# Moving the large SBUF buffers by 160 bytes, and the feed-forward's small pool behind its others, in a one-core streaming-encoder block

## The chip, the cores and the metric

The kernel runs on one core of one Trainium2 chip. The metric is the device time of one execution in microseconds (us). Before the change it is 2313.43 us, the median of three runs (2312.34 to 2315.29).

## The reference

One layer of an encoder trunk on a sequence of 1024 tokens of width 1024, all in fp32. A combined projection feeds two recurrent branches (RWKV-7 and HGRN2), whose gated sum is projected and added to the tokens; then come cross-attention to 256 memory tokens, a SwiGLU feed-forward with 2816 hidden columns, and a last norm. Cut to what the change touches:

```python
    h = h + (gate_a * y_a + gate_b * y_b) @ w_out[l]
    ...
    o = jnp.einsum('bhqm,bmhd->bqhd', p, v).reshape(B, S, D_MODEL)
    h = h + o @ xa_wo[l]

    u = rmsnorm(h, norm_ffn_g[l])
    h = h + (jax.nn.silu(u @ ffn_w1[l]) * (u @ ffn_w3[l])) @ ffn_w2[l]
return rmsnorm(h, norm_final_g)
```

## The kernel before, in words

**Products.** Each large product is taken with operands split into a high and a low part of type fp32r: `split` (L282 writes the high part on ScalarE, L286 the low part on GpSimd or VectorE). `mm3` (L299 to L302) issues three matmuls for each pair of blocks: high by high, low by high, high by low. In the profile an operation `P<-ah,whT` of L300 has the result P, the moving operand ah (512 columns of 4 bytes, so 2048 bytes of each partition) and the stationary operand whT (128 columns, 512 bytes). The mixing part's instructions are recorded through one helper, so they all stand at L103.

**Stages.** The mixing part (projections pproj, the two recurrences) takes the first 1300 us or so. Then come keys and values of the memory (pk, pvv), the output projection and cross-attention (pq, psc, po, pw) up to 1663 us, and from there the feed-forward with the final norm.

**End of attention.** `add_project` multiplies by `xa_wo`, adds the result to the tokens tok (VectorE, L1796), squares them for the next norm (ScalarE, L1799) and stores each of the last four token tiles to the scratch tensor h_d (L1801, a DMA that SyncE, SP, issues). These four tiles lie in 4096-byte buffers of attention's ring hp; the last buffer of that ring spans bytes 174,240 to 178,336 of each partition.

**Feed-forward.** The first layer's 2 x 2 block product is done with seven products instead of eight (P1 to P7) for each of 11 blocks f and the two matrices w1 and w3; one product is 12 matmuls (`product`). P5 and P4 of f = 0, 1 and 2 use only the first half of the tokens, which is normalized already, so they come right behind attention's last projection (`early_products`): 12 products, read as `P<-ah,whT`, `P<-al,whT` and `P<-ah,wlT`. Their weights come in 256-KB loads (`raw`, L1969, on SP's DMA queue) into the tile wraw, 10 buffers: 8 loads for each f, in the order A0[0], A1[0], A0[2], A1[2], ... (`weights(f, True)`). `behind` lets the scheduler set the loads of f = 0 no earlier than the eighth-last load of `xa_wo`, and those of f = 1 no earlier than the last. `early_operands` takes differences of them on VectorE (L2080, L2083, L2084) and splits each into whT (ScalarE, L282) and wlT (GpSimd, L286). The operand of the first product, T1[0], needs the loads 1 and 3. `late_blocks` loads the other half of the tokens back from h_d into hn (L1998), takes its norm (ssn: L1999 and `rstd`, L276 and L277; hn: L2003), and loads the sums s and b (L2005, L2006), before it transposes. The second layer (acc<-wh,th and the like) follows from the scratch tensors.

**Order.** The tile framework schedules the instructions of every engine by priorities and by its own estimate of when operands and buffers are free; each engine, and the SP queue, then works strictly in that order. A tile of a new pool that lies over a tile of a pool that was closed has to wait until that old tile's last use (the pools of `tpool` with `reuse_waits="tile"`).

**Addresses.** A pool gets its bytes when it is opened, behind the pools that are open. The moving operands of 2048 bytes start at these remainders of a division by 2048: uh, ah, whi and those of the same pools at 1888, the feed-forward's tl, th, wh and wl at 224. The stationary rows of 512 bytes start at 352 (the first group) and at 224 (the second) beyond a multiple of 512. The feed-forward's pools are opened in the order f_s (2432 bytes: ssn, ssf, junkf), f_t (tl, th), f_f (u2, u3, c, kept), f_w (wraw, wh, wl). Its first wraw buffer starts at byte 178,400, just behind the last buffer of attention's ring hp.

Of the kernel before, what the change touches and what calls it, by code (L numbers as in the profile page):

```python
# [10 lines left out]
F32 = mybir.dt.float32  # L11
# [7 lines left out]
P = 128  # L19
# [165 lines left out]
def tile_trunk(ctx, tc, x, mem, norm_mix_g, w_in, rw_mu, rw_w0, rw_w2, rw_a0, rw_a2, rw_g2,  # L185
# [5 lines left out]
    def tpool(**kw):  # L191

        return tc.tile_pool(reuse_waits="tile", **kw)

    const = ctx.enter_context(tc.tile_pool(name="const", bufs=1))
    dram = ctx.enter_context(tc.tile_pool(name="dram", bufs=1, space=DRAM))

    def behind(ins, name):

        tc.add_manual_dep(ins, name, mybir.DependencyInfo(mybir.DependencyClass.NoSync, mybir.DependencyReason.DATA),  # L200
                          reason="order")
# [137 lines left out]
    def scratch(name, shape):  # L339
        return dram.tile(shape, F32, name=name)  # L340
# [1615 lines left out]

    sp = ctx.enter_context(tpool(name="f_s", bufs=2))
    ring = ctx.enter_context(tpool(name="f_t", bufs=20))  # L1960
    fp = ctx.enter_context(tpool(name="f_f", bufs=2))
    wp = ctx.enter_context(tpool(name="f_w", bufs=1))
    pp = ctx.enter_context(tpool(name="f_p", bufs=8, space=PSUM))
    hd = scratch("hid_d", [FT, NHALF, P, HALF])
    hsd = scratch("hsum_d", [4, HF, P, HALF])
# [363 lines left out]
```

## Time and profile before

| what | value |
|---|---|
| median of three runs | 2313.43 us (2312.34 to 2315.29) |
| the profiled execution, first to last instruction (span) | 2308.0 us, 5.4 us below the median |
| TensorE (PE) busy | 2270.0 us, 98% of the span, 18,262 matmuls |
| VectorE, ScalarE, GpSimd busy | 68%, 49%, 45% |
| mean granted TensorE clock | 0.998 |
| PE in the 48 us up to 1665 us | 48.00 us busy |
| DMA share in the same 48 us | 0.98 of the 16 engines, 287 GB/s |
| loads of feed-forward weights (L1969) | 145, 256 KB each |

The time beside the span is read as a constant: what lies around the first and the last instruction. In a window's row stand the busy time of PE, PE's weight loads, VectorE, ScalarE and GpSimd with their instructions, then the granted TensorE clock, the share of time in which the 16 DMA engines moved data, and GB/s. In a row of the timeline stand the start, the duration, the engine, the line, the operation, the tiles and, in brackets, the idle time just before it and what ended it; for SP the duration is the time to issue the transfers. Matmuls are pipelined: each shows some 390 ns, but the next one starts some 230 ns later.

### The profile page before, as it was taken

Reading aid. Unit: us, or ns where it says so; the run is one execution under the profiler, and the core shown is the slowest. Engines: PE = TensorE matmul, PEld = TensorE weight load, DVE = VectorE, ACT = ScalarE, POOL = GpSimd, SP = SyncE. Lnnn points to the kernel's source line nnn. Section 1 sums busy time; section 2 is a strip of 40 time slices with the busy share of each in tenths; the row PEclk is TensorE's granted clock in tenths of the full one; section 3 lists DMA queues with packets and bytes.
Section 4 is the critical chain, followed back from the end, with each engine's and each line's share of the span. In section 5 each row is a group of like instructions: output and inputs, shape, how many; then the busy total and the mean of one; then the engine's idle time right before and its main releaser. Section 6 shows DMA issues by size and latency. Waiting matters only on the chain.

```text
span 2308.0 us, 47067 instructions
## 1 busy us (share of the span) xinstructions
PE 2270.0 (98%) x18262; PEld 1860.1 (81%) x18262; DVE 1558.0 (68%) x2513; ACT 1134.2 (49%) x2259; POOL 1037.3 (45%) x1129
## 2 busy tenths in 40 slices
PE   7999999999999999999999999999999999999998
PEld 5788887787888887888788888888888888888887
DVE  5788874666777757776766566555778665566655
ACT  6545454545565656564566424443453333334533
POOL 3555555555565655575566100000266655551212
PEclk9999999999999999999999999999999999999999
DMA  5444445233334244434334897117933433348653
GB/s 174 119 134 123 131 122 171 69 102 85 88 103 122 75 120 112 134 82 116 92 90 123 286 348 264 55 56 261 290 121 117 132 96 110 96 158 305 207 172 120
DMA packets 393691, 327.94 MB, mean 142 GB/s; under 512 B 107595, under 2 KB 318653, under 8 KB 392061
## 3 DMA queue, kind: packets, MB, share of 16 engines
q1 hardware_dynamic: 391549, 319.17, 45.4%
q0 software_dynamic: 1344, 4.72, 0.5%
q8 instruction: 144, 2.36, 0.4%
q10 hardware_dynamic: 576, 1.05, 0.1%
q14 instruction: 78, 0.64, 0.1%
HBM read 228.12 MB, written 96.21 MB: 141 GB/s over the span
## 4 chain that ended last, share of the span: by engine, by line
PE 73%; DVE 4%; DMA 3%; POOL 2%; issue 1%; ACT 1%; SPq 0%; POOLq 0%; ACTq 0%; DVEq 0%
PE pproj L103 21%; PE P L301 6%; PE P L302 6%; PE P L300 6%; PE acc L301 3%; PE acc L302 3%; PE acc L300 3%; PE pw L302 3%; PE pw L301 2%; PE pw L300 2%; PE cm L103 2%; PE psA L103 2%; PE psc L103 1%; PE po L103 1%; PE pq L301 1%
## 5 line engine op out<-in xcount | busy, mean ns | idle before, releaser
L103 PE MATMUL pproj<-uh,whi 128*128 128x512 f32 x768 | 320.0, 417 | 0.7 <-DVE q L103 0.7
L103 PE MATMUL pproj<-uh,wlo 128*128 128x512 f32 x768 | 300.9, 392 | 2.7 <-POOL wlo L103 2.3
L103 PE MATMUL pproj<-ul,whi 128*128 128x512 f32 x768 | 301.5, 393 | 0.0
L286 POOL TENSOR_TENSOR wl<-wraw,wh 128x512 fp32r<-128x512 f32 x87 | 121.4, 1402 | 199.8 <-ACT wh L282 171.7
L103 POOL TENSOR_TENSOR wlo<-wraw,whi 128x512 fp32r<-128x512 f32 x96 | 128.4, 1348 | 118.4 <-ACT whi L103 111.2
L300 PE MATMUL pproj<-uh,whi 128*128 128x512 f32 (+1 forms) x432 | 177.4, 411 | 1.1 <-ACT uh L328 0.7
L282 ACT ACTIVATE whi<-wraw 128x512 fp32r<-128x512 f32 (+1 forms) x166 | 100.9, 617 | 156.3 <-PE pw L302 73.6
L103 PEld LDWEIGHTS pproj<-uh,whi 128*128 128x128 f32 x768 | 144.5, 188 | 34.0 <-DVE q L103 2.0
L302 PE MATMUL pproj<-uh,wlo 128*128 128x512 f32 (+1 forms) x432 | 170.0, 394 | 1.8 <-POOL wlo L286 1.8
L103 PEld LDWEIGHTS pproj<-ul,whi 128*128 128x128 f32 x768 | 144.4, 188 | 32.3
L301 PE MATMUL pproj<-ul,whi 128*128 128x512 f32 (+1 forms) x432 | 169.6, 393 | 0.0
L103 PEld LDWEIGHTS pproj<-uh,wlo 128*128 128x128 f32 x768 | 145.0, 189 | 28.1 <-POOL wlo L103 2.8
L277 POOL TENSOR_TENSOR ss<-ss,nhalf 128x4 f32<-128x4 f32 (+1 forms) x7 | 6.2, 881 | 323.1 <-DMA wraw<-in_xa_wo_dram 186.6
L286 POOL TENSOR_TENSOR wlT<-wraw,whT 128x512 fp32r<-128x512 f32 x72 | 102.0, 1424 | 85.1 <-ACT whT L282 73.7
L282 ACT ACTIVATE wh<-wraw 128x512 fp32r<-128x512 f32 x143 | 87.0, 623 | 92.3 <-PE P L301 69.1
L286 DVE TENSOR_TENSOR wlo<-wraw,whi 128x512 fp32r<-128x512 f32 x134 | 93.1, 701 | 55.3 <-ACT whi L282 53.4
L103 ACT ACT_TABLE_LOAD x90 | 115.5, 1283 | 14.3 <-DVE m L103 7.2
L301 PE MATMUL acc<-wl,th 128*128 128x512 f32 x308 | 119.9, 389 | 0.0
L302 PE MATMUL acc<-wh,tl 128*128 128x512 f32 x308 | 119.8, 389 | 0.0
L300 PE MATMUL acc<-wh,th 128*128 128x512 f32 x308 | 119.8, 389 | 0.0
L2273 DVE TENSOR_TENSOR tl<-tl,th 128x512 fp32r<-128x512 f32 x77 | 60.1, 792 | 63.6 <-ACT th L2272 63.2
L300 PE MATMUL pw<-whi,ah 128*128 128x512 f32 x256 | 100.6, 393 | 1.2 <-ACT whi L282 0.7
(457 smaller groups left out, 6383.0 us busy)
## 6 DMA issues: line engine op xcount, KB each, us to landing
wraw<-in_w_in_dram SPq DMA_DIRECT2D x148, 256.0 KB
wraw<-in_ffn_w_dram SPq DMA_DIRECT2D x145, 256.0 KB
y<-in_ffn_w_dram SPq DMA_DIRECT2D x22, 512.0 KB
wsum_d<-y SPq DMA_DIRECT2D x11, 1024.0 KB
hsum_d<-s SPq DMA_DIRECT2D x44, 256.0 KB
tl<-hsum_d SPq DMA_DIRECT2D x44, 256.0 KB
wraw<-wsum_d SPq DMA_DIRECT2D x44, 256.0 KB
hid_d<-s SPq DMA_DIRECT2D x33, 256.0 KB
```

The costliest lines, as they stand in the source:

```text
L103: r = getattr(self.engine, op)(*a, **kw)
L277: nc.gpsimd.tensor_tensor(dst, tmp, nhalf[:, 0:n], op=ALU.pow)
L282: nc.scalar.activation(hi, src, AF.Copy)
L286: e.tensor_tensor(lo, src, hi.bitcast(F32), op=ALU.subtract)
L300: nc.tensor.matmul(ps, ah, bh, start=first, stop=False)
L301: nc.tensor.matmul(ps, ah, bl, start=False, stop=False)
L302: nc.tensor.matmul(ps, al, bh, start=False, stop=last)
L2273: tt(hl, hl.bitcast(F32), hh.bitcast(F32), op=ALU.subtract)
```

## The change

Two edits. A tile of 160 bytes named align, which nothing reads, is the first of the const pool, so that everything behind it moves up by 160 bytes: uh from byte 20,320 to 20,480, which is 10 times 2048. And the pool f_s is opened as the last of the feed-forward's four SBUF pools instead of the first, so that the three others begin 2432 bytes lower; with the 160 bytes that makes 2272 bytes: tl from 55,520 to 53,248, the first wraw buffer from 178,400 to 176,128, wh from 198,880 to 196,608. After it, of the 512-column moving operands those at 1888 and 224 lie at 0 beyond a multiple of 2048 (7620 matmuls of the program), and the stationary rows belonging to them at 0 beyond a multiple of 512. The last buffer of attention's ring hp now spans 174,400 to 178,496, and the first two wraw buffers (176,128 to 180,224) lie partly over it.

```diff
+    const.tile([P, 40], F32, name="align")
...
-    sp = ctx.enter_context(tpool(name="f_s", bufs=2))
     ring = ctx.enter_context(tpool(name="f_t", bufs=20))
     fp = ctx.enter_context(tpool(name="f_f", bufs=2))
     wp = ctx.enter_context(tpool(name="f_w", bufs=1))
+    sp = ctx.enter_context(tpool(name="f_s", bufs=2))
```

No instruction is added or removed, but the scheduler's order differs from about 1617 us on, and nowhere earlier. All lines behind L196 count two more after the change (L1969 becomes L1971).

The queue of SP at the end of attention's last projection, before the change: L1770 loads `xa_wo`, L1969 loads feed-forward weights, L1801 stores the tokens, L1998 loads them back.

```order
L1770 DMA wraw<-in_xa_wo_dram 128x512
L1969 DMA wraw<-in_ffn_w_dram 128x4x128 x8
L1770 DMA wraw<-in_xa_wo_dram 128x512 x6
L1823 DMA early_d<-sums 128x512
L1770 DMA wraw<-in_xa_wo_dram 128x512
L1969 DMA wraw<-in_ffn_w_dram 128x4x128 x8
...
L1969 DMA wraw<-in_ffn_w_dram 128x4x128 x6
L1801 DMA h_d<-tok 128x1024 x3
L1998 DMA hn<-h_d 128x512
L1801 DMA h_d<-tok 128x1024
L1998 DMA hn<-h_d 128x512 x7
```

Left out between the two pieces are the rest of 29 such weight loads (8, 8, 3, 2, 1, 1 and 6) and stores to early_d; all 29 stand ahead of the stores of the tokens.

The same place of the same queue after the change (L1772, L1971, L1803 and L2000 are those lines).

```order
L1772 DMA wraw<-in_xa_wo_dram 128x512 x8
L1825 DMA early_d<-sums 128x512
...
L1803 DMA h_d<-tok 128x1024 x3
L2000 DMA hn<-h_d 128x512
L1803 DMA h_d<-tok 128x1024
L2000 DMA hn<-h_d 128x512 x3
L1971 DMA wraw<-in_ffn_w_dram 128x4x128 x16
L2000 DMA hn<-h_d 128x512 x4
```

The first weight load of the feed-forward now stands behind all four stores of the tokens and behind four of the eight loads hn; its wait is for the third of those stores to have landed and for ScalarE's squares (L1799) of the last tiles.

VectorE at the same place before the change: L286 makes the last low parts of attention, L2080, L2083 and L2084 take the differences of weights (here those of f = 1; those of f = 0 stand further up), L1796 adds the projection to the tokens.

```order
L286 TENSOR_TENSOR al<-sums,ah 128x512
L2080 TENSOR_TENSOR wraw<-wraw 128x512 x2
L2083 TENSOR_TENSOR wraw<-wraw 128x512 x2
L2084 TENSOR_TENSOR wraw<-wraw 128x512 x2
L1796 TENSOR_TENSOR tok<-pw,tok 128x512 x4
L1999 TENSOR_REDUCE ssn<-ssq 128x4
L276 TENSOR_SCALAR ssn<-ssn 128x4
L2003 TENSOR_SCALAR hn<-hn,ssn 128x512 x8
```

And VectorE after the change.

```order
L288 TENSOR_TENSOR al<-sums,ah 128x512
L1798 TENSOR_TENSOR tok<-pw,tok 128x512 x4
L2001 TENSOR_REDUCE ssn<-ssq 128x4
L278 TENSOR_SCALAR ssn<-ssn 128x4
L2005 TENSOR_SCALAR hn<-hn,ssn 128x512 x4
L2082 TENSOR_TENSOR wraw<-wraw 128x512 x2
L2085 TENSOR_TENSOR wraw<-wraw 128x512 x2
L2086 TENSOR_TENSOR wraw<-wraw 128x512 x2
```

The differences of f = 0 and of f = 1 now stand behind the last additions to the tokens and behind four scalings of hn; ScalarE's splits into whT and GpSimd's into wlT have moved with them. PE's order is the same as before: the last matmul of pw, then the early products P.

## The prediction

> **What bounds the kernel now.** I read the page first: its busy times and the shares of the chain that ended last.
>
> ```profile
> span 2308.0 us, 47067 instructions
> PE 2270.0 (98%) x18262; PEld 1860.1 (81%) x18262; DVE 1558.0 (68%) x2513; ACT 1134.2 (49%) x2259; POOL 1037.3 (45%) x1129
> PE 73%; DVE 4%; DMA 3%; POOL 2%; issue 1%; ACT 1%; SPq 0%; POOLq 0%; ACTq 0%; DVEq 0%
> ```
>
> TensorE is busy for 98% of the span and carries 73% of the chain. So two things can move the time: how fast matmuls follow one another, and whether PE is left without operands. Next the busy times by stage: the end of attention, the hand-over to the feed-forward, and stretches of the feed-forward.
>
> ```profile
> 1617.00:1665.00 48.00, 48.00 (x228) 39.86 (x227) 38.61 (x56) 23.91 (x48) 12.02 (x8) 1.00 0.98 287
> 1665.00:1677.00 12.00, 12.00 (x53) 9.74 (x52) 5.49 (x11) 4.48 (x8) 6.18 (x5) 1.00 0.94 330
> 1677.00:1700.00 23.00, 23.00 (x117) 19.08 (x116) 16.34 (x24) 14.98 (x27) 15.49 (x11) 1.00 0.43 131
> 1700.00:1900.00 200.00, 199.08 (x874) 163.55 (x873) 146.96 (x170) 68.70 (x119) 124.73 (x88) 1.00 0.35 109
> 1900.00:2100.00 200.00, 200.00 (x877) 164.25 (x875) 116.24 (x149) 68.47 (x113) 101.26 (x77) 1.00 0.42 137
> ```
>
> PE has no gap across the hand-over (48.00 of 48, 12.00 of 12, 23.00 of 23), at full clock, while the DMA engines move 287 to 330 GB/s. From 1700 us on it is idle for 0.92 us in 400. So whatever PE loses at the hand-over is not caught up behind it: there is no later wait that would shrink.
>
> How the gap is avoided stands in the timelines: first SP's queue, then three rows of VectorE, then PE, ScalarE and GpSimd.
>
> ```profile
> 1617.57 7.03 SPq L1969 DMA_DIRECT2D wraw<-in_ffn_w_dram  x8
> 1634.65 5.79 SPq L1969 DMA_DIRECT2D wraw<-in_ffn_w_dram  x8
> 1653.94 6.02 SPq L1969 DMA_DIRECT2D wraw<-in_ffn_w_dram  x6
> 1660.19 2.15 SPq L1801 DMA_DIRECT2D h_d<-tok  x3
> 1665.09 0.32 SPq L1998 DMA_DIRECT2D hn<-h_d  x1
> 1665.50 0.38 SPq L1801 DMA_DIRECT2D h_d<-tok  x1
> 1665.94 4.37 SPq L1998 DMA_DIRECT2D hn<-h_d  x7
> ```
>
> ```profile
> 1640.56 0.69 DVE L2080 TENSOR_TENSOR wraw<-wraw 128x512 f32<-128x512 f32 x1 [2.27 <-DMA wraw<-in_ffn_w_dram]
> 1663.35 0.69 DVE L1796 TENSOR_TENSOR tok<-pw,tok 128x512 f32<-128x512 f32 x1 [1.35 <-PE pw L302]
> 1668.28 0.49 DVE L2003 TENSOR_SCALAR hn<-hn,ssn 128x512 f32<-128x512 f32 x1 [3.02 <-DMA hn<-h_d]
> ```
>
> ```profile
> 1662.91 0.40 PE L302 MATMUL pw<-whi,al 128*128 128x512 f32 x1
> 1663.15 0.40 PE L300 MATMUL P<-ah,whT 128*128 128x512 f32 x1
> 1665.94 0.39 PE L300 MATMUL P<-ah,whT 128*128 128x512 f32 x1
> ```
>
> ```profile
> 1665.97 0.63 ACT L282 ACTIVATE whT<-wraw 128x512 fp32r<-128x512 f32 x1 [1.11 <-PE P L301]
> 1666.68 1.29 POOL L286 TENSOR_TENSOR wlT<-wraw,whT 128x512 fp32r<-128x512 f32 x1 [0.27 <-ACT whT L282]
> ```
>
> Feed-forward weights are loaded 46 us ahead of use, beside attention's last projection, and the first early product starts at 1663.15, 0.24 us after the last pw. These early products were put there to fill the time in which h_d is stored, loaded back and normalized (1660.19 to past 1668.28).
>
> **The change part by part: the hand-over.** After the change all feed-forward weight loads stand on SP behind the four stores h_d and the first four loads hn, and VectorE, ScalarE and GpSimd have moved with them. PE's order is unchanged, so PE stands at the first P until the weights for it are loaded, subtracted and split. Queued behind the waiting SP instruction are 16 weight loads, four hn, then s and b; behind the waiting matmul is all of the feed-forward. Step by step:
>
> 1. The last add to the tokens ends at 1663.35 + 0.69 = 1664.04; it can't be earlier, as pw runs as before. The first hn waits for the first store to land. Before, that took 1665.09 − 1660.19 = 4.9 us, behind six weight loads issued up to 1659.96; an hn load itself takes 1668.28 − 1665.09 = 3.2 us from issue to use. So the first hn goes out at 1663.4 to 1665.1 and the fourth store at 1664.04 to 1665.5.
> 2. Behind it three hn (4.37 / 7 = 0.62 us each, 0.44 for the store): first weight load at 1666.3 to 1667.8. The first product needs loads 1 and 3, and a load takes 5.79 / 8 = 0.72 us to issue: load 3 at 1667.8 to 1669.2.
> 3. From issue to use: at least the 3.2 us of hn; at most what the third load of the batch at 1634.65 took to the subtraction at 1640.56, 4.5 us. That gives 1671.0 to 1673.7.
> 4. Subtraction 0.69 and split 0.63: PE starts at 1672.3 to 1675.0 instead of 1663.15, so it stands for 9.2 to 11.9 us.
> 5. The third matmul needs wlT, 1.29 us behind whT, of which two matmuls at half clock cover some 0.85; with the hand-over between engines 0.4 to 0.8 us.
>
> Standing has a price of its own, the clock. The one wait of PE over 2 us in the mixing part and the windows around it:
>
> ```profile
> 406.00 0.39 PE L103 MATMUL pproj<-uh,whi 128*128 128x512 f32 x1
> 408.04 0.39 PE L103 MATMUL pproj<-uh,whi 128*128 128x512 f32 x1
> 410.77 0.79 PE L103 MATMUL pproj<-uh,wlo 128*128 128x512 f32 x1 [2.34 <-POOL wlo L103]
> 411.00:415.00 4.00, 4.00 (x14) 3.25 (x15) 0.09 (x1) 1.34 (x3) 1.63 (x2) 0.60 0.72 150
> 415.00:425.00 10.00, 10.00 (x48) 8.28 (x47) 8.10 (x13) 9.52 (x16) 8.64 (x13) 1.00 0.53 130
> ```
>
> After 2.34 us of idling the clock is 0.60 over the next 4 us and 1.00 after them: 4 × 0.40 = 1.6 us lost. Here PE idles four times as long; I take 1.6 as the low end and twice that and a little, 3.4, as the high one, 2.0 as the value. The Trainium skill ("TensorE: Matmul & The Clock Gate", "What's actually happening") has the clock halved after an idle window of about 3.4 us and restored after as long a busy one; by that rule a window at half clock costs, as an estimate, 1.7 us, and the trace agrees in size, though here 2.34 us of idling sufficed.
>
> 6. The weights of f = 2 come later as well: 16 weight loads, 8 hn, and s and b are 32 transfers of 256 KB or 8.4 MB, 25 us at 330 GB/s, beside the 8 products of 12 × 232.5 ns that f = 0 and 1 give to cover it, 22 us. I take 0 to 4 us, 1.5 as the value, since before, the DMA engines were already at 0.94 in this stretch.
>
> Sum of what is added: low 9.2 + 0.4 + 1.6 + 0 = 11.2 us, high 11.9 + 0.8 + 3.4 + 4 = 20.1, and with the middle values 10.6 + 0.6 + 2.0 + 1.5 = 14.7.
>
> **The change part by part: the addresses.** What alignment does to a matmul must come from rows with operands that lie differently today.
>
> ```profile
> L300 PE MATMUL P<-ah,whT x176: 390/393/477, 1663.1 to 2084.3; 128*128 128x512 f32 x176
> L300 PE MATMUL P<-hB,wh x176: 389/389/495, 1700.0 to 2062.3; 128*128 128x512 f32 x176
> L698 PE MATMUL pg<-sgh,g2s x16: 391/394/497, 379.9 to 397.2; 96*128 96x512 f32 x16
> L300 PE MATMUL pk<-mT,whi x48: 277/283/283, 1305.6 to 1333.5; 128*128 128x256 f32 x48
> L103 PE MATMUL pproj<-uh,whi 128*128 128x512 f32 x768 | 320.0, 417 | 0.7 <-DVE q L103 0.7
> L300 PE MATMUL pproj<-uh,whi 128*128 128x512 f32 (+1 forms) x432 | 177.4, 411 | 1.1 <-ACT uh L328 0.7
> L300 PE MATMUL acc<-wh,th 128*128 128x512 f32 x308 | 119.8, 389 | 0.0
> L300 PE MATMUL pw<-whi,ah 128*128 128x512 f32 x256 | 100.6, 393 | 1.2 <-ACT whi L282 0.7
> ```
>
> And two matmuls of 256 columns, pk, with 24 more between them:
>
> ```profile
> 1330.21 0.28 PE L300 MATMUL pk<-mT,whi 128*128 128x256 f32 x1
> 1333.21 0.28 PE L301 MATMUL pk<-mT,whi 128*128 128x256 f32 x1
> ```
>
> The pace is the distance of starts: (408.04 − 406.00) / 9 = 226.7 ns for pproj, whose moving operand is at 1888 of 2048, and (1665.94 − 1663.15) / 12 = 232.5 ns for the early products. The one thing that sets the latter apart is that ah (1888) and whT (224) differ by more than a multiple of 256; hB and wh, both at 224, show a shorter duration, 389 instead of 393. So what these rows reward is that moving and stationary rows lie alike, which 224 with 224 and 1888 with 352 (both 96 beyond a multiple of 256) do already. After the change ah and whT are alike too: 528 matmuls (3 × 176) × 5.8 ns = 3.1 us gained. The bounds: 0 if it isn't the address, and 3.1 if it is; I take 3.1, since the two paces and the durations of these products fit it. For the others I take 0: they change from alike to alike.
>
> **Sum.** 14.7 − 3.1 = 11.6 us more; the bounds are 11.2 − 3.1 = 8.1 and 20.1. The profiled execution has a span of 2308.0, 5.4 us below the median of 2313.4 of the runs; the same 5.4 is put on the span after: 2308.0 + 11.6 + 5.4 = 2325.0 us, its own range 2319 to 2334 (the bounds of the sum, 2321.5 to 2333.5, and 2 us below).
>
> **The rivals.**
>
> *Aligned rows stream faster.* A moving row on a multiple of 2048 could be worth something in itself; this ends on the other side. pk starts every (1333.21 − 1330.21) / 25 = 120 ns; by the slope between 256 and 512 columns, 512 columns take (226.7 − 120) × 2 = 213.4 ns, so 13.3 ns of each matmul isn't columns. If that were rows crossing a boundary of 2048 bytes, it would be won back in the 3 × (768 + 432 + 308 + 256) + 1848 = 7140 matmuls (1848 for the first layer of the feed-forward: 11 × 7 × 2 products of 12): 95 us, for 2313.4 + 14.7 − 95 = 2233 us (the 3.1 are part of it). It overtakes the hand-over from 11.6 / 7140 = 1.6 ns a matmul on.
>
> Against it: a row of 256 columns, which crosses such a boundary half as often at most, keeps the same 13.3; offsets 224 and 1888 cross it at opposite ends of a row and run alike; and g2s, whose moving rows lie on multiples of 128, is no shorter (394). For it: no moving row of 512 columns lies on a multiple of 2048 today, so nothing shows the case itself. The Trainium skill ("TensorE: Matmul & The Clock Gate", "Back-to-back issue gap") gives N / 2.4 + 2.5 ns for matmuls alone, an estimate of 215.8 ns here; if alignment were what this kernel lacks to it, 10.9 × 7140 = 78 us would go and the time would be 2250; no run here shows a pace below 226.7, and the trace's weight load before each matmul is the simpler reason. Chance 0.16.
>
> *Aligned rows collide.* Moving and stationary rows that start at the same remainder of 2048, and those of the other engines too, might meet in the memory. Before, the spread from best to worst alike-ness was 5.8 ns; at 1 to 6 ns on 7140 matmuls that is 7 to 43 us, on top of the hand-over 2332 to 2368. For it only that addresses do matter (393 against 389); against it that pairs alike in the low 8 bits are the fast ones. Chance 0.07.
>
> *The hand-over is hidden after all, or the change does nothing.* If stores land at once and the weights arrive while the h_d work still runs, PE would stand for 3 us or less, with 3.1 gained from ah: 2311 to 2317. Against it is the order, which puts the weights behind the last add. Chance 0.05.
>
> **Chances.** The hand-over as worked out has 0.72: 2325.0. A difference of 0.2%, 4.6 us, is about what a measurement of this kernel can tell from none. Faster by more: the first rival and a trifle, 0.17. Within: the third rival and the low tail of the forecast, 0.08. Slower: 0.75. The range leaves out the first rival (0.16) and the far end of the second: 2311 (the third rival's low end) to 2348, which takes in a collision of up to 3 ns.
>
> **What would show it.** In the changed profile's timeline SP issues wraw<-in_ffn_w_dram only after 1664 us; PE's first `P<-ah,whT` carries an idle time of 9 to 12 us ended by ACT whT; the clock of the next 4 us is near 0.6; no other stage of PE idles more than before; early products show 389 instead of 393; and the ends of the mixing part and of attention keep their times. If pproj's starts are closer than 226.7 ns, or the feed-forward ends earlier though the idle time is there, the first rival holds and the forecast is wrong; if they are farther apart, the second.

## The result, and the profile after

The changed kernel takes 2329.4 us (median of five runs, 2328.04 to 2332.14) against 2312.34 for the kernel before (five runs); the ratio is 1.0078, with a 95% interval of 1.0067 to 1.0089, so some 18 us slower. The profiled execution has a span of 2327.3 us, 19.3 more than before. In the experiments below one of the eleven executions with 128 bytes alone took 7837.34 us; that kernel's ratio leaves it out.

The busy times by stage, in the windows that were shown of before (busy time of PE, weight loads, VectorE, ScalarE and GpSimd, then clock, DMA share and GB/s):

```profile
1617.00:1665.00 48.00, 46.22 (x220) 38.24 (x219) 24.33 (x39) 20.27 (x41) 1.01 (x1) 1.00 0.39 141
1665.00:1677.00 12.00, 1.91 (x4) 1.10 (x5) 5.39 (x9) 1.26 (x2) 3.03 (x3) 0.62 1.03 315
1677.00:1700.00 23.00, 23.00 (x98) 18.91 (x97) 18.15 (x20) 10.01 (x18) 10.57 (x8) 0.90 1.02 330
1700.00:1900.00 200.00, 194.39 (x855) 160.12 (x854) 150.88 (x169) 74.18 (x130) 133.43 (x91) 0.97 0.36 113
1900.00:2100.00 200.00, 200.00 (x884) 165.58 (x884) 126.41 (x155) 67.62 (x113) 111.12 (x84) 1.00 0.37 119
```

PE's 12 us from 1665 on, full before, hold 1.91 us of work at a clock of 0.62. The DMA engines are at 0.39 up to 1665 us, where they were at 0.98, and saturated behind it: the weights that came early now come late. The fourth row shows more: 194.39 busy instead of 199.08, at 0.97. There is a second wait behind 1700 us.

SP's queue (start, time to issue), and the first use of the weights on VectorE and on ScalarE:

```profile
1657.85 4.40 SPq L1803 DMA_DIRECT2D h_d<-tok  x3
1662.36 0.37 SPq L2000 DMA_DIRECT2D hn<-h_d  x1
1663.97 0.32 SPq L1803 DMA_DIRECT2D h_d<-tok  x1
1664.34 1.77 SPq L2000 DMA_DIRECT2D hn<-h_d  x3
1666.20 13.89 SPq L1971 DMA_DIRECT2D wraw<-in_ffn_w_dram  x16
```

```profile
1673.54 1.50 DVE L2082 TENSOR_TENSOR wraw<-wraw 128x512 f32<-128x512 f32 x2 [1.81 <-DMA wraw<-in_ffn_w_dram]
```

```profile
1674.27 0.63 ACT L284 ACTIVATE whT<-wraw 128x512 fp32r<-128x512 f32 x1 [9.51 <-DVE wraw L2082]
```

And PE: the first early product, its slow followers, nine matmuls at the new pace, the second wait, and a product well behind both.

```profile
1674.95 0.79 PE L302 MATMUL P<-ah,whT 128*128 128x512 f32 x1 [11.74 <-ACT whT L284]
...
1677.33 0.63 PE L303 MATMUL P<-al,whT 128*128 128x512 f32 x1
...
1680.74 0.63 PE L302 MATMUL P<-ah,whT 128*128 128x512 f32 x1
...
1681.55 0.39 PE L304 MATMUL P<-ah,wlT 128*128 128x512 f32 x1
1681.78 0.39 PE L302 MATMUL P<-ah,whT 128*128 128x512 f32 x1
...
1683.82 0.39 PE L302 MATMUL P<-ah,whT 128*128 128x512 f32 x1
...
1716.45 0.39 PE L304 MATMUL P<-hB,wl 128*128 128x512 f32 x1
1721.14 1.22 PE L302 MATMUL P<-hB,wh 128*128 128x512 f32 x2 [4.31 <-ACT hB L2023]
...
1724.94 0.79 PE L303 MATMUL P<-lB,wh 128*128 128x512 f32 x1 [1.30 <-DVE lB L2024]
...
1806.89 0.39 PE L302 MATMUL P<-hB,wh 128*128 128x512 f32 x1
```

The matmuls at 1716.45 and 1806.89 are these two of before, by their number in PE's order:

```profile
1701.96 0.39 PE L302 MATMUL P<-hB,wl 128*128 128x512 f32 x1
...
1784.59 0.39 PE L300 MATMUL P<-hB,wh 128*128 128x512 f32 x1
```

From such pairs the delay of PE at each place can be read. At the first early product it is 1674.95 − 1663.15 = 11.8 us. At the 13th it is 1680.74 − 1665.94 = 14.8: the eight matmuls from 1677.33 on start 427 ns apart, near twice the usual, and the two up to 1681.55 lose another 0.3, which makes 15.1. Ahead of the second wait it is 1716.45 − 1701.96 = 14.5, at 1806.89 it is 22.3, and at the end of the span 19.3. So the ledger is 11.8 for the wait, 3.3 for the slow matmuls and the late wlT, −0.6 within the early products, 7.8 for the second wait and what follows it, and −3.0 over the rest.

The early products win a part back: their pace is now (1683.82 − 1681.78) / 9 = 226.7 ns, and their duration has become that of the others (minimum, median, maximum in ns):

```profile
L302 PE MATMUL P<-ah,whT x176: 389/389/792, 1675.0 to 2104.0; 128*128 128x512 f32 x176
```

### The profile page after: what moved, and what is told of

Same layout as the page of the kernel before. It is cut to its first block, busy times and chain, and to the rows that moved or that the text cites. A ratio compares the mean times of both kernels' runs of the same rounds, so it can differ in the third digit from the quotient of the medians.

```text
span 2327.3 us, 47067 instructions
## 1 busy us (share of the span) xinstructions
PE 2273.3 (98%) x18262; PEld 1864.7 (80%) x18262; DVE 1569.6 (67%) x2513; ACT 1133.8 (49%) x2259; POOL 1038.8 (45%) x1129
```

## The experiments

The theory was: the move of f_s alone makes the loss, because wraw then lies over attention's last token tiles; the pace of matmuls depends only on whether moving and stationary rows are alike in their low address bits; a multiple of 2048 is worth nothing. The first rival: aligned rows are faster, and their gain hides behind a larger loss.

**The two edits apart.**

```diff
 only_align:  + const.tile([P, 40], F32, name="align")
 only_pool:   - sp = ... f_s            (ahead of f_t)
              + sp = ... f_s            (behind f_w)
```

> The 160 bytes alone; the pool f_s stays first. The order of all engines is that of before; the operands up to the end of attention lie on multiples of 2048, the feed-forward's at 384 beyond one, so ah and whT differ by 128 beyond a multiple of 256, as before. Theory (the pool's move makes the stall, and only the likeness of moving and stationary rows in the low 8 bits sets the pace): same time as before, ratio 1.000 within 0.001, no wait at the first early product, early products still 232 to 233 ns apart. Rival (a row on a multiple of 2048 is worth something in itself, and its gain hides in the result behind a larger loss): the stages up to 1663 us get shorter, by 5 us or more for 1 ns a matmul.

Measured: ratio 0.9993 (0.9985 to 1.0002), and in a second run beside two others 0.9998 (0.9989 to 1.0007).

> The 160 bytes alone again. Theory: ratio 1.000. Rival (the 160 bytes bring something of their own): ratio 0.9993 or less, with an interval that ends below 1.000.

Its early products are as slow as before (tile P in the first of the two runs):

```profile
L302 PE MATMUL P<-ah,whT x176: 390/393/478, 1661.1 to 2081.3; 128*128 128x512 f32 x176
```

With attention and the mixing part on multiples of 2048 nothing that the runs can tell is won.

> The pool's move alone, without the 160 bytes. All operands of 2048 bytes lie at 1888 beyond a multiple of 2048, the feed-forward's too; order of all engines as after the change. Theory: the same as after the change, ratio to before 1.0078 within 0.001: PE stands for 11 to 12 us before the first early product, some 14 matmuls then start 427 ns apart, the later early products 226.7 ns apart, and a second wait comes at hB near 1717 us. Rival (multiples of 2048 are worth something): slower than after the change by 5 us or more, and early products that keep 232 ns.

Measured: ratio 1.0086 (1.0072 to 1.0099), 2328.68 us: the changed kernel's time without one row on a multiple of 2048. PE and tile P of it:

```profile
1675.49 0.79 PE L301 MATMUL P<-ah,whT 128*128 128x512 f32 x1 [11.98 <-ACT whT L283]
...
1721.79 1.22 PE L301 MATMUL P<-hB,wh 128*128 128x512 f32 x2 [4.29 <-ACT hB L2022]
```

```profile
L301 PE MATMUL P<-ah,whT x176: 387/389/794, 1675.5 to 2104.7; 128*128 128x512 f32 x176
```

Both waits and the faster early products come with the pool's move; all operands are then at 1888, alike among themselves. This is against the first rival in both halves.

**How little overlap it takes.**

```diff
+    const.tile([P, 40], F32, name="align")
...
+    ctx.enter_context(tpool(name="f_pad", bufs=1)).tile([P, 224], F32, name="pad")
     sp = ctx.enter_context(tpool(name="f_s", bufs=2))
...
-        junk = sp.tile(..., tag="junkf", name="junkf", bufs=2)
+        junk = sp.tile(..., tag="junkf", name="junkf", bufs=1)
```

> The 160 bytes, f_s first again but 1024 bytes smaller (one buffer junkf instead of two), and 896 unused bytes ahead of it, so that the feed-forward's first wraw buffer begins at 178,432: it lies over the last 64 bytes of attention's ring instead of the 2368 of the change. Rows of the feed-forward at 256 beyond a multiple of 2048, those of attention at 0, alike in the low 8 bits, not in the low 9. The order on SP is that of after the change. Theory (any overlap of wraw with the last token tiles makes all its loads late): as after the change, ratio 1.0078 within 0.0015, with a wait of 11 to 12 us before the first early product. And if likeness counts in the low 8 bits, early products 226.7 ns apart; if in the low 9, 232 ns. Rival (f_s at the end, or the place of tl and th, makes the wait): ratio 1.000 or below.

Measured: ratio 1.0073 (1.0059 to 1.0087). PE's first early product, and its tile P:

```profile
1674.06 0.80 PE L302 MATMUL P<-ah,whT 128*128 128x512 f32 x1 [11.09 <-ACT whT L284]
```

```profile
L302 PE MATMUL P<-ah,whT x176: 389/389/795, 1674.1 to 2102.5; 128*128 128x512 f32 x176
```

With f_s in its old place, 64 bytes of overlap do what 2368 do in the changed kernel, within what the ratios tell. The first load of the ring is queued behind the four stores of the tokens here too (SP issues it at 1666.07, against 1666.20 in the changed kernel), and the others stand behind it. The early products take 389 ns at addresses that agree in the low 8 bits but differ by 256, while the pairs that lie 128 apart (the early products before) and 64 apart (po, below) are the slow ones. So likeness counts modulo 256.

**The gain without the wait.** 128 bytes ahead of the feed-forward's pools make its rows like ah and leave wraw behind attention's ring; so do 160 and 128 bytes together, with attention on multiples of 2048.

```diff
 pad128, both_high:
+    ctx.enter_context(tpool(name="f_pad", bufs=1)).tile([P, 32], F32, name="pad")
     sp = ctx.enter_context(tpool(name="f_s", bufs=2))
 both_high alone:
+    const.tile([P, 40], F32, name="align")
```

> Before with 128 unused bytes ahead of the feed-forward's pools: its operands lie at 352 beyond a multiple of 2048, so that ah (1888) and whT (352) are alike in the low 8 bits (96), while nothing lies on a multiple of 2048, and wraw stays behind attention's ring. Theory: the order of before, no wait, early products 226.7 instead of 232.5 ns apart, so 528 x 5.8 ns = 3.1 us faster than before, ratio 0.9987. Rival (only multiples of 2048 help): ratio 1.000 and 232.5 ns.

> The 160 bytes, and 128 more ahead of the feed-forward's pools with f_s still first: attention and mixing part on multiples of 2048, the feed-forward at 512 beyond one, all alike in the low 9 bits, wraw behind attention's ring. Theory: the order of before, no wait, early products 226.7 ns apart, ratio 0.9987, the same as with 128 bytes alone. Rival (multiples of 2048 help): faster than with the 128 bytes alone by 5 us or more.

> The 128 bytes ahead of the feed-forward's pools again, beside the next two on one chip. Theory (only likeness in the low 8 bits counts): ratio 0.9987, as both_high_again. Rival (the 160 bytes bring something of their own): slower than both_high_again by 2 us or more.

> The 160 and the 128 bytes again. Theory: ratio 0.9987, as pad128_again. Rival (the 160 bytes bring something of their own): ratio 0.9975 or less.

Measured: the 128 bytes 0.9989 (0.9980 to 0.9998) and again 0.9990 (0.9982 to 0.9999); both 0.9972 (0.9962 to 0.9982) and again 0.9979 (0.9970 to 0.9988). Both are faster than before, and the early products are at 389 ns in each; here in the second run of both:

```profile
L302 PE MATMUL P<-ah,whT x176: 389/389/478, 1661.9 to 2078.7; 128*128 128x512 f32 x176
```

The theory had 0.9987 for each. It fits the 128 bytes; for both together it lies outside the first interval and just inside the second. Both together came out 2.5 to 4 us better than the 128 bytes alone in both pairs of runs, which is the sign that the rival named ahead of the second pair (2 us or more), though the intervals overlap by 0.0002 and 0.0006. A part of it can be seen: with the 128 bytes alone PE waits at hB in both profiles, here in the second, and with both it doesn't.

```profile
1701.50 0.50 PE L300 MATMUL P<-hB,wh 128*128 128x512 f32 x1 [1.06 <-ACT hB L2022]
1702.29 0.50 PE L301 MATMUL P<-lB,wh 128*128 128x512 f32 x1 [0.28 <-DVE lB L2023]
```

That is 1.3 us. The kernel before waits 0.9 us at the same place, and the one with the 160 bytes alone 0.3 us in both of its profiles. Why the 160 bytes take it away, and whether the rest is theirs, stays open; the 160 bytes alone were 0.5 to 1.6 us faster than before, but both of their intervals take in 1.000.

**Everything alike.**

```diff
         sp = xctx.enter_context(tpool(name="small", bufs=2))
+        sp.tile([P, 48], F32, name="align2", bufs=1)
```

> The kernel with 160 and 128 bytes and f_s first, and 192 unused bytes in attention's small pool, so that attention's ring, keys and act2 move up by 192 bytes: 189 matmuls of pw and 88 of po, which had moving and stationary rows 64 apart, are now alike in the low 8 bits. wraw begins at 178,688, the very end of attention's ring. Theory: the order of before, no wait; 277 x 6 = 1.7 us less than with the 160 and 128 bytes alone, ratio 0.9965; pw at 226.7 ns throughout. Rival (likeness counts only for the early products): no change in pw, ratio 0.9972.

Measured: ratio 0.9973 (0.9962 to 0.9983), 2303.52 us. The 1.7 us can't be told from the runs, but the mechanism can be read in po, which had moving and stationary rows 64 apart: before (the kernel with 160 and 128 bytes shows a median of 394 as well), and in this kernel,

```profile
L300 PE MATMUL po<-pTh,Vh x32: 392/394/398, 1456.8 to 1575.9; 128*128 128x512 f32 x32
```

```profile
L302 PE MATMUL po<-pTh,Vh x32: 389/389/389, 1457.4 to 1576.3; 128*128 128x512 f32 x32
```

**What the first wait costs beside its idle time.** Filling it with matmuls holds the clock up:

```diff
+    fill = psum("fill")
+    for _ in range(48):
+        nc.tensor.matmul(fill, fa[0][:, 0, 0:P], fa[0][:, 0, :], start=True, stop=True)
```

> After the change, with 48 matmuls of 512 columns on ready operands ahead of the first early product, into a PSUM tile that nobody reads; they add work and leave none out. Theory (the wait costs its idle time and, on top of it, the clock): the first early product starts where it did, PE is busy before it, no matmul at 427 ns behind it, so 14 x 0.2 = 2.8 to 3.4 us are won against after, ratio about 1.0064. Rival (the slow start behind the wait comes from operands that are late): the early products keep their distances and the time is that of after or longer.

Measured: ratio 1.0082 (1.0069 to 1.0096), the time of the changed kernel as far as the ratios tell. PE:

```profile
1662.59 11.04 PE L2150 MATMUL fill<-ah 128*128 128x512 f32 x48
1674.19 0.50 PE L302 MATMUL P<-ah,whT 128*128 128x512 f32 x1 [0.56 <-ACT whT L284]
1675.55 0.50 PE L304 MATMUL P<-ah,wlT 128*128 128x512 f32 x1 [0.62 <-POOL wlT L288]
...
1713.55 0.39 PE L304 MATMUL P<-hB,wl 128*128 128x512 f32 x1
...
1718.61 0.49 PE L302 MATMUL P<-hB,wh 128*128 128x512 f32 x1 [4.68 <-ACT hB L2023]
1722.39 0.79 PE L303 MATMUL P<-lB,wh 128*128 128x512 f32 x1 [3.29 <-DVE lB L2024]
...
1804.91 0.39 PE L302 MATMUL P<-hB,wh 128*128 128x512 f32 x1
```

The slow early products are gone (0.50 us instead of 0.79 at the first, a clock of 1.00 instead of 0.50 from 1675 to 1679 us), and ahead of the second wait PE's delay is 1713.55 − 1701.96 = 11.6 us instead of 14.5. Half a microsecond of this gain of 2.9 was there before the hand-over. At hB and lB a part is given back: PE waits 4.68 + 3.29 = 8.0 us instead of 4.31 + 1.30 = 5.6, and behind it the delay is 1804.91 − 1784.59 = 20.3 us instead of 22.3. So 2.0 us are left in this profile, and the runs show none of them. The theory's 2.8 to 3.4 us missed, and its rival had the time right for a wrong reason: it was the clock that slowed those matmuls, but hB and lB, which come from other engines, took up a part of what PE had won.

**What makes the second wait.** VectorE of the changed kernel there, from 1698 us:

```profile
1698.10 1.28 DVE L2082 TENSOR_TENSOR wraw<-wraw 128x512 f32<-128x512 f32 x2
...
1701.17 2.81 DVE L2086 TENSOR_TENSOR wraw<-wraw 128x512 f32<-128x512 f32 x2
...
1711.53 1.78 DVE L2115 TENSOR_TENSOR wraw<-wraw 128x512 f32<-128x512 f32 x1
...
1719.11 0.74 DVE L2028 SCALAR_TENSOR_TENSOR fS<-pth,VC,fS 128x512 f32<-128x512 f32 x1
```

and ScalarE, which works in order too:

```profile
1719.88 0.63 ACT L284 ACTIVATE hS<-fS 128x512 fp32r<-128x512 f32 x1 [1.08 <-DVE fS L2028]
1720.42 1.25 ACT L2023 ACTIVATE hB<-pth,VC 128x512 fp32r<-128x512 f32 x2
```

hB stands behind hS on ScalarE, and hS waits for VectorE, which between the four steps of the late half now takes the six weight differences of f = 2 and the six of the first full block, f = 0. Before, those of f = 2 were done by 1660 us. Those of f = 0 ran from 1676.94 on; the last of them began at 1689.59, ahead of PE's first use of hB at 1700.03. These are the last of each in the kernel before:

```profile
1658.88 0.69 DVE L2084 TENSOR_TENSOR wraw<-wraw 128x512 f32<-128x512 f32 x1 [0.48 <-DMA wraw<-in_ffn_w_dram]
1689.59 1.78 DVE L2114 TENSOR_TENSOR wraw<-T,wraw 128x512 f32<-128x512 f32 x1
```

In the changed kernel those of f = 0 run from 1709.00 to 1724.23, and take 9.6 us in sum where they took 5.2 before; what stretches them was not tested. Two runs leave the differences out:

```diff
-            tt(a21, a21, a11, op=ALU.subtract)     (and L2085, L2086; for f = 2)
...
         for a11, a12, a21, a22 in A:
+            if f == 0:
+                continue                            (nosub20 alone: L2116 to L2118 of f = 0)
```

> After the change, without the six subtractions and additions of weights for f = 2 (L2082, L2085, L2086): the early products of f = 2 take the raw weights, so that part of the result is left out. Theory (the second wait, 4.3 us at hB near 1717 us, comes because these six, which before were done by 1660 us, now stand on VectorE between the four steps of the late half of the tokens): the wait at hB falls below 1 us and its slow matmuls go, 6 to 8 us less than after, ratio about 1.0048. Rival (the later transfers of hn, s and b make it): the wait stays as it is and the time is that of after.

Measured: ratio 1.0064 (1.0051 to 1.0078). The wait has shrunk, not gone:

```profile
1717.73 0.49 PE L302 MATMUL P<-hB,wh 128*128 128x512 f32 x1 [3.42 <-ACT hB L2023]
```

That fell short of the theory (below 1 us, and a ratio of 1.0048, which lies outside the interval), and the rival's unchanged wait doesn't fit either. By PE's delay the place costs 4.4 us instead of 7.8. So the other six were taken out as well.

> After the change, without the six subtractions for f = 2 and also without the six of the first full block (f = 0: L2116 to L2118), so that part of the result is left out. Theory (VectorE's weight differences, which before were done ahead, now stand between the steps of the late half and hold up hB): the wait at hB, 3.4 us without the first six, falls below 1 us, no slow matmuls behind it; 3 to 4 us less than without the first six alone, ratio about 1.0048. Rival (GpSimd's splits or late transfers hold hB): the wait stays above 3 us and the ratio at 1.0064.

Measured: ratio 1.0039 (1.0026 to 1.0053). The engines from 1717 to 1721 us, first in the changed kernel, where PE stood, then in this one; then PE at the one wait that is left in the hand-over, and at the first matmul of the step at which the changed kernel waited a second time:

```profile
1717.00:1721.00 4.00, 0.00 (x0) 0.00 (x0) 4.00 (x5) 2.86 (x6) 4.00 (x4) 0.76 0.45 132
1717.00:1721.00 4.00, 4.00 (x19) 3.30 (x18) 2.07 (x2) 1.86 (x4) 4.00 (x4) 1.00 0.24 67
```

```profile
1674.07 0.80 PE L302 MATMUL P<-ah,whT 128*128 128x512 f32 x1 [11.43 <-ACT whT L284]
...
1714.77 0.39 PE L302 MATMUL P<-hB,wh 128*128 128x512 f32 x1
```

The second wait is wholly gone, with the first product and the weight loads as late as in the changed kernel and GpSimd as busy (4.00 of 4.00). It was VectorE's work, and it took all twelve operations to make it: without them the time is (1.0078 − 1.0039) × 2312 = 9 us shorter. Not all of these 9 us are part of the 18, since the kernel before has some of the six of f = 0 between the steps of its late half too, and waits 0.9 us at hB itself. By PE's delay this kernel gains 1.5 us there against before, where the changed kernel loses 7.8.

## Why the prediction was right, and where its terms were off

**The hand-over (steps 1 to 4).** Right in place, cause and size. The first hn went out at 1662.36, a microsecond ahead of its range, which won nothing, as the fourth store (1663.97) still had to wait for the last add. The first weight load was issued at 1666.20, just ahead of the forecast's 1666.3 to 1667.8. It shows no wait of its own there: SP came straight from the loads of hn (1664.34 + 1.77 = 1666.11), so it was its place in the queue that made it late, and the overlap, by the runs, that gave it this place. The third went out near 1666.20 + 2 × 13.89 / 16 = 1667.9 and was used at 1673.54, 5.6 us later, more than the 4.5 taken as the most: 16 loads issued in a row share the DMA engines, which have no pause in that stretch (a DMA share of 1.03). The end of it, 1673.54 and PE at 1674.95, is at the upper edge of what was worked out, and the wait is 11.7 us against 9.2 to 11.9.

**The late wlT and the clock (step 5 and what follows it).** Forecast 0.6 + 2.0, measured 3.3 together, within the bounds. The price isn't a fixed one: by the delay of the 15th early product less that of the first, the four other profiles with such a wait show 3.4 (only_pool), 1.9 (overlap64), 2.5 (nosub2) and 2.3 us (nosub20). And the run with filler matmuls shows that the term doesn't simply add up: with the clock held up, the loss at the second wait grew from 7.8 to 8.7 us. How much of the clock's price the whole time carries stays open, between the 2.0 us of that profile and the nothing of its runs.

**The weights of f = 2 (step 6).** The step that failed. It priced late transfers at 0 to 4 us, 1.5 as the value. PE lost 7.8 us, behind the early products at hB, and not through transfers: without twelve operations of VectorE the wait is gone, though the loads come as late. Six of them (f = 2) had been done beside attention's last projection, the other six (f = 0) ahead of PE's first use of hB; after the change all twelve stand in the stretch in which VectorE has the late half of the tokens to do. The forecast says that VectorE's work moved, and the order shown with the change has the differences of f = 0 and 1 behind hn, but only the DMA side of the move got a price. Of the signs that the prediction lists, the one that failed is this: no other stage of PE idles more than before.

**The addresses.** Right: 528 matmuls at 226.7 instead of 232.5 ns. The forecast was 3.1 us; of the changed kernel's delay 0.6 us goes within the early products of f = 0 to 2, and 3.0 behind 1806.89, half a microsecond more than the forecast, of which the origin isn't shown. The kernels without the wait are 2.3 to 6.5 us faster than before, by the ratios.

**The sum.** 11.6 us forecast, 17 by the medians, 18 by the ratio and 19.3 by the span. By the span 7.7 us are missing: 6.3 at the second wait (7.8 instead of 1.5), 1.2 at the first (11.8 instead of 10.6), 0.7 for wlT and the clock (3.3 instead of 2.6), less 0.5 that the addresses won beyond their 3.1. That 2325.0 comes nearer to 2329.4 than this is luck: 5.4 us were put on the span as what lies around it, but in every run for which both are on record the time is only 1.7 to 2.1 us above the span (2329.4 − 2327.3 = 2.1 here), which made the forecast 3.3 us too long. 2329.4 lies within the forecast's own range, 2319 to 2334, and would lie within it, near its end, with 2.1 as well.

**The rivals.** Aligned rows don't stream faster: 0.9993 and 0.9998 with attention and mixing aligned, and the same loss with no row aligned (1.0086). At its break-even of 1.6 ns, the 3 × (768 + 432 + 256) = 4368 matmuls ahead of the feed-forward would have given the 160 bytes 7 us, a ratio of 0.9970, outside both intervals. The rule of the Trainium skill that was weighed with it ("TensorE: Matmul & The Clock Gate", "Back-to-back issue gap"), for matmuls alone, gives an estimate of 215.8 ns for 512 columns. No run here reaches it: every matmul comes with a weight load, and 226.7 ns is the pace of the fast products, aligned or not. Aligned rows don't collide either: the same 389 ns at 0, 256, 352 and 512 beyond a multiple of 2048. And the wait wasn't hidden.

## What to carry to other kernels

A few bytes in one pool can decide what another pool lies over, and with it when the first load of a whole ring may start; in a queue that works in order, 64 bytes of overlap cost as much as 2368 (ratios of 1.0073 and 1.0078). Before moving pools, compare the order of the DMA queue and of the vector engines around the stage boundary, and price every engine whose work moved, not the transfers alone. If alignment is wanted, put the padding where it pushes the early loads away from the old stage's last buffers: here 160 and 128 bytes made all these rows alike without the wait, at a ratio of 0.9972 to 0.9979.

## What the runs showed of the hardware

The pace of a matmul with weight load depends on the addresses of its operands against each other: 226.7 ns where the moving and the stationary rows agree modulo 256, 232.5 ns where they lie 128 apart (the early products before; a single matmul of them shows 393 ns instead of 389). Where they lie 64 apart, po shows 394 ns instead of 389. The place in a row of 2048 bytes makes no difference: 389 ns at 0, 256, 352 and 512. And a PE that waits 11.7 us pays with 14 slow matmuls behind it, most of them 427 ns apart, in windows at a clock of 0.62 and 0.90. In the five profiles with a wait of 11.1 to 12.0 us this price, with that of the late wlT, is 1.9 to 3.4 us; whether it costs time is decided by what is late next.
